# Feed-forward operands made in the stage ahead, half by half; two lead pairs; the position rows written in eight copies

## The chip, the cores and the metric

The kernel runs on one core of one Trainium2 chip. The metric is the device time of one execution in microseconds (us). The kernel before takes 2559.06 us, the median of 3 runs (2556.69 to 2561.37). Below, the engines are PE (matrix products), DVE (VectorE), ACT (ScalarE), POOL (GpSimd) and SP (SyncE, whose queue issues every DMA of this kernel).

## The reference

Two transformer blocks on x of 1024 positions by 1024 channels, in fp32. What the change touches is the end of the first block's cross attention, its feed-forward layer, and two small preparations of the second block that are done beside it:

```python
x = x + o @ w_co                               # cross attention's output projection
h = rmsnorm(x, norm_ffn)
gate, up = split(h @ w_gu, 2)                  # 22 tiles of 128 columns each
x = x + (silu(gate) * up) @ w_down             # hidden width 2816
x = rmsnorm(x, final_norm)
# second block, prepared beside the feed-forward layer:
ada = silu(c) @ ada_w + ada_b                  # 8 vectors of 1024 values
pos_bias = rel_bias[buckets]                   # 16 heads, by distance, masked
```

## The kernel before

Every fp32 product is made as three products of a high and a low part (`wh`/`wl` of the weights, `Xh`/`Xl` or the two `R` of the operand): three matmuls of 128x128 by 128x512. ACT copies the high part, DVE subtracts it for the low part (`split`, and L251/L252 for weights). The 1024 positions are two halves `hf` of 512.

**The co projection** (`g_dense(cow...)`): half 0 for 8 tiles of channels (woven into the cross attention), then half 1. `Residual` adds each result to x (DVE, L1186), squares it on ACT and sums the squares; `rstd()` turns the sum into 1/rms: 4 small matmuls, a power on POOL, 4 matmuls that spread it over the partitions, a copy on ACT (`rf[hf]`).

**Gate and up tile 0** (`g_gu0`) take x times the gain, not yet normalised (`raw_split`, made for half 0 beside the co projection of half 1), and multiply by `rf` when the result is read out.

**Tiles 1 to 21 of gate and up** (`g_fast`) are 21 pairs (gate tile, up tile) by two halves of the input channels and of the positions: a 2x2 block product made with 7 products (A11, A12, S2, S1, S3, A22, S4) of 12 matmuls instead of 8. Their right sides are the blocks B11, B21, B12, B22 of the normalised x and the sums T1 to T4, each split into high and low: `g_operands0`, `g_operands1` (sums on POOL, `right_sums`) and `g_operands2`. Their left sides are weight blocks and their sums (`fast_operand`), made two products ahead per buffer (3 buffers, `ahead`). `load_fast` loads a pair's two weight tiles.

**Beside these products** runs `mods`, one step after each product (`mix`, L1577): first `g_sliding_bias`, then 16 times `g_modulation` (8 loads of `araw`, 8 multiply-adds on DVE into `aacc`, 4 transposes on PE, one reduction). What is left of `mods` after the last product runs by itself (L1578). `g_sliding_bias` makes a table of 16 heads by 384 distances (16 partitions), adds the mask (L1377) and writes every head's row 128 times to `d_bs` in DRAM, in one DMA of 3 MB (L1378). It is read back eight stages later.

`hidden` stores the hidden tiles and their sums in DRAM (`d_h`) for the down projection `dn0` to `dn2`, which has the same 7-product form. Before it, x is loaded again (L1584) and the first third of its operands is fetched and split (`fetch`, `place`).

**What sets the order:** the program is recorded in the order of these generators; a scheduler then places the instructions of each engine's queue by its own estimate of what is ready when. Each engine, and SP's queue, then works in that fixed order and waits at an instruction whose inputs or buffers aren't there. The pool `v` (`vtile2`) has NV = 20 tiles, shared by part of the operands, the hidden tiles and sums, `araw` and `aacc`, and the table of `g_sliding_bias`.

## Time and profile before

| | |
|---|---|
| median of 3 runs | 2559.06 us |
| the profiled execution | 2555.8 us, of it 2553.8 us span |
| PE busy | 2387.7 us (93%) |
| DVE, ACT, POOL busy | 1733.6, 1069.4, 635.6 us |
| DMA | 252.34 MB, 99 GB/s on average |

The profile is of one execution. PE is the engine that is busy nearly all the time, so time that PE stands idle or runs at the lower clock is what a change can take away or add. [...]

### The profile page before, as it was taken

Reading aid. Unit: us, or ns where it says so; the run is one execution under the profiler, and the core shown is the slowest. Engines: PE = TensorE matmul, PEld = TensorE weight load, DVE = VectorE, ACT = ScalarE, POOL = GpSimd, SP = SyncE. Lnnn points to the kernel's source line nnn. Section 1 sums busy time; section 2 is a strip of 40 time slices with the busy share of each in tenths; the row PEclk is TensorE's granted clock in tenths of the full one; section 3 lists DMA queues with packets and bytes.
Section 4 is the critical chain, followed back from the end, with each engine's and each line's share of the span. In section 5 each row is a group of like instructions: output and inputs, shape, how many; then the busy total and the mean of one; then the engine's idle time right before and its main releaser. Section 6 shows DMA issues by size and latency. Waiting matters only on the chain.

```text
span 2553.8 us, 33162 instructions
## 1 busy us (share of the span) xinstructions
PE 2387.7 (93%) x11726; PEld 1976.9 (77%) x11726; DVE 1733.6 (68%) x3238; ACT 1069.4 (42%) x2214; POOL 635.6 (25%) x593
## 2 busy tenths in 40 slices
PE   8899979998997699999699989999999998999997
PEld 7789967777875588888488867888888886788876
DVE  6325667887688577777898675454644658788765
ACT  5214665765653233333344453121221224566652
POOL 4004555534205122221000120000000006544443
PEclk9999988999998899999799989999999999999999
DMA  4322223433242754455754211111111121111123
GB/s 159 95 79 94 63 51 105 123 100 124 73 143 67 172 175 161 158 179 184 275 176 138 75 33 58 42 58 50 43 41 58 50 66 50 59 51 58 60 91 118
DMA packets 122937, 252.34 MB, mean 99 GB/s; under 512 B 21380, under 2 KB 36404, under 8 KB 122772
## 3 DMA queue, kind: packets, MB, share of 16 engines
q1 hardware_dynamic: 122772, 250.24, 31.2%
q8 instruction: 92, 1.51, 0.3%
q14 instruction: 73, 0.60, 0.1%
HBM read 199.84 MB, written 50.33 MB: 98 GB/s over the span
## 4 chain that ended last, share of the span: by engine, by line
PE 77%; DVE 8%; DMA 5%; issue 3%; ACT 3%; POOL 3%; SPq 0%; DVEq 0%; POOLq 0%; ACTq 0%
PE wd L356 11%; PE wd L364 11%; PE wd L363 11%; PE fx L1444 4%; PE fx L1446 4%; PE fx L1445 4%; PE mm L356 2%; PE mm L363 2%; PE mm L364 2%; PE tp L760 2%; PE op L775 2%; PE fz L1444 2%; PE fz L1446 2%; PE fz L1445 2%; DMA wraw<-in_w_in_f 2%
## 5 line engine op out<-in xcount | busy, mean ns | idle before, releaser
L356 PE MATMUL wd<-Xh,wh 128*128 128x512 f32 x756 | 298.7, 396 | 5.1 <-ACT Xh L334 2.1
L364 PE MATMUL wd<-Xl,wh 128*128 128x512 f32 x756 | 295.8, 395 | 7.6 <-DVE Xl L335 7.6
L363 PE MATMUL wd<-Xh,wl 128*128 128x512 f32 x756 | 296.0, 392 | 1.3 <-POOL wl L263 1.3
L263 DVE TENSOR_TENSOR wl<-wraw,wh 128x1024 fp32r<-128x1024 f32 (+1 forms) x121 | 150.5, 1251 | 206.8 <-ACT wh L262 205.9
L262 ACT ACTIVATE wh<-wraw 128x1024 fp32r<-128x1024 f32 (+2 forms) x157 | 158.1, 1013 | 283.7 <-issue 139.6
L428 POOL TENSOR_TENSOR nr<-nv,half 128x4 f32<-128x4 f32 (+1 forms) x25 | 26.7, 1072 | 771.3 <-DVE nv L422 762.1
L1446 PE MATMUL fx<-R,wh 128*128 128x512 f32 x480 | 189.1, 397 | 10.5 <-DVE R L335 10.4
L1444 PE MATMUL fx<-R,wh 128*128 128x512 f32 x480 | 188.6, 398 | 7.8 <-ACT R L334 7.4
L1445 PE MATMUL fx<-R,wl 128*128 128x512 f32 x480 | 190.4, 397 | 0.0
L364 PEld LDWEIGHTS wd<-Xl,wh 128*128 128x128 f32 x756 | 142.6, 189 | 41.6 <-DVE Xl L335 10.0
L356 PEld LDWEIGHTS wd<-Xh,wh 128*128 128x128 f32 x756 | 142.5, 189 | 36.7 <-ACT Xh L334 3.5
L363 PEld LDWEIGHTS wd<-Xh,wl 128*128 128x128 f32 x756 | 142.6, 189 | 33.0 <-POOL wl L263 2.0
L1188 DVE SCALAR_TENSOR_TENSOR x<-wd,ada,x 128x512 f32<-128x512 f32 x144 | 106.4, 748 | 78.0 <-PE wd L364 78.0
L335 DVE TENSOR_TENSOR ptl<-tp,pth 128x512 fp32r<-128x512 f32 (+2 forms) x196 | 122.8, 635 | 50.5 <-ACT pth L334 48.1
L396 POOL TENSOR_TENSOR acc<-acc,sq 128x512 f32<-128x512 f32 (+1 forms) x49 | 72.2, 1475 | 277.4 <-ACT sq L395 265.6
L760 PE MATMUL tp<-ident,p 128*128 128x128 f32 x712 | 122.8, 284 | 11.2 <-POOL p L704 6.8
L334 ACT ACTIVATE pth<-tp 128x512 fp32r<-128x512 f32 (+2 forms) x196 | 106.8, 557 | 54.2 <-PE tp L760 33.9
L1446 PEld LDWEIGHTS fx<-R,wh 128*128 128x128 f32 x480 | 91.3, 190 | 32.4 <-DVE R L335 12.6
L1444 PE MATMUL fz<-R,wh 128*128 128x512 f32 x240 | 95.9, 400 | 21.8 <-DVE c L1555 21.8
L1444 PEld LDWEIGHTS fx<-R,wh 128*128 128x128 f32 x480 | 91.6, 191 | 29.1 <-ACT R L334 8.3
L1400 DVE SCALAR_TENSOR_TENSOR aacc<-araw,cact,aacc 128x512 f32<-128x512 f32 x112 | 95.9, 856 | 25.6 <-DMA araw<-in_ada_w 24.2
L251 ACT ACTIVATE wh<-ws 128x512 fp32r<-128x512 f32 (+1 forms) x132 | 73.8, 584 | 90.5 <-PE fx L1446 62.4
(374 smaller groups left out, 6786.9 us busy)
## 6 DMA issues: line engine op xcount, KB each, us to landing
araw<-in_ada_w SPq DMA_DIRECT2D x128, 256.0 KB, 4.2
wraw<-in_a_w_in SPq DMA_DIRECT2D x34, 512.0 KB, 3.5
hr<-d_h SPq DMA_DIRECT2D x63, 256.0 KB, 4.0
wraw<-in_w_gu SPq DMA_DIRECT2D x23, 512.0 KB, 4.7
sraw<-in_w_gu SPq DMA_DIRECT2D x21, 512.0 KB, 3.6
d_h<-H SPq DMA_DIRECT2D x36, 256.0 KB, 2.7
wraw<-in_a_w_out SPq DMA_DIRECT2D x18, 512.0 KB, 3.5
x<-d_x SPq DMA_DIRECT2D x32, 256.0 KB, 4.8
```

Source lines behind the costliest of these rows:

```text
L262: A.activation(out=wh[:, sl], in_=raw[:, sl], func=AF.Copy)
L263: (G if pool_split[0] else V).tensor_tensor(out=wl[:, sl], in0=raw[:, sl], in1=wh[:, sl].bitcast(F32), op=ALU.subtract)
L334: A.activation(out=h, in_=src, func=AF.Copy)
L335: V.tensor_tensor(out=l, in0=src, in1=h.bitcast(F32), op=ALU.subtract)
L356: ins = T.matmul(ps, lhsT=wh, rhs=xh, start=start, stop=False)
L363: T.matmul(ps, lhsT=wl, rhs=xh, start=False, stop=False)
L364: T.matmul(ps, lhsT=wh, rhs=xl, start=False, stop=stop)
L760: T.transpose(tp[:, (o + j) * 128:(o + j + 1) * 128], b, ident)
L1188: V.scalar_tensor_tensor(out=xt(f, hf), in0=ps, scalar=self.gate(f), in1=xt(f, hf), op0=ALU.mult, op1=ALU.add)
L1444: T.matmul(ps, lhsT=wh[:, sl], rhs=rh[k], start=new and k == 0, stop=False, skip_group_check=not new)
L1445: T.matmul(ps, lhsT=wl[:, sl], rhs=rh[k], start=False, stop=False, skip_group_check=not new)
L1446: T.matmul(ps, lhsT=wh[:, sl], rhs=rl[k], start=False, stop=k == nk - 1, skip_group_check=not new)
```

## The change

- `fast_order(npair, lead)` gives the order of the products; with lead 2 the gate/up stage begins with A11 and A12 of pairs 0 and 1, which need B11 and B21 alone.
- `g_operands0` normalises half 0 of x and makes B11 and B21 beside the co projection of half 1. `g_gu0` uses these for half 0, so half 0's raw split is gone; half 1's raw split and both spills of x follow each result of the co projection. The sum of squares of half 1 goes to POOL.
- T1 and T2 are made on DVE, T3 and T4 on POOL, beside `g_gu0` and the first four products.
- The table of the position rows has a tile of its own (`mk`); NV is 19. Its rows are written two heads at a time, by eight DMAs, recorded ten steps of `mods` apart.
- A step of `mods` after each product and a second one after every third; a modulation has 10 steps instead of 11.
- Beside the last pairs: the first operands of the down projection are fetched and split, and x is loaded again (`done_gu`, `x_again`).

```diff
+    def fast_order(npair, lead=1):
+        seq = [(i, o) for i in range(lead) for o in ("A11", "A12")]
+        for i in range(npair):
+            seq += [(i, o) for o in ("A12", "S2", "S1", "S3") if (i, o) not in seq]
+            if lead <= i + 1 < npair:
                 seq.append((i + 1, "A11"))
+            elif i + 1 < lead:
+                seq.append((i + 1, "S2"))
             seq += [(i, "A22"), (i, "S4")]
...
-                if op == "A12":
-                    load_fast(key[0], key[1] + 1)
+                if op == "A12" and key[1] == 0:
+                    load_fast(key[0], 1)
+                elif op == "S4":
+                    load_fast(key[0], key[1] + 2)
...
-    NV = 20
+    NV = 19
...
+        res.nm[1].eng = G
+        res.raw = lambda f, hf: nc.sync.dma_start(out=d_x[:, f, hs(hf)], in_=xt(f, hf))
...
-        run(weave(g_dense(cow[1], seqB, 4, Xo, res), bg=[g_raw_split(0, gf, X)], every=4))
...
+        mk = ff.tile([16, 384], F32, name="mk")
...
-            V.tensor_tensor(out=bv, in0=psb[:16, :384], in1=bv, op=ALU.add)
-            nc.sync.dma_start(out=d_bs, in_=bv.rearrange("h (o t) -> h o t", o=1).to_broadcast([16, 128, 384]))
+            V.tensor_tensor(out=mk, in0=psb[:16, :384], in1=mk, op=ALU.add)
+        def g_bias_rows():
+            for h in range(0, 16, 2):
+                nc.sync.dma_start(out=d_bs[h:h + 2], in_=mk[h:h + 2].rearrange("h (o t) -> h o t", o=1)
+                                  .to_broadcast([2, 128, 384]))
+                for _ in range(10):
+                    yield 0.0
...
             for k in range(8):
                 norm(k, 0)
-                if k >= 4:
-                    put("B21", k, xt(k, 0))
+                put("B11" if k < 4 else "B21", k, xt(k, 0))
                 yield 0.0
         def g_operands1():
             for k in range(4):
+                b = bs[k]
+                norm(k, 1)
+                b["T1"], b["T2"] = vtile2("T1"), vtile2("T2")
+                V.tensor_tensor(out=b["T1"], in0=b["B12"], in1=b["B11"], op=ALU.subtract)
+                yield 0.0
+                norm(k + 4, 1)
+                V.tensor_tensor(out=b["T2"], in0=b["B22"], in1=b["T1"], op=ALU.subtract)
+                yield 0.0
+                put("T2", k, b["T2"])
                 yield 0.0
...
-        run(mix(g_fast("gu", 21, 4, R, evac_gu), mods, 1))
+        run(weave(g_dense(cow[1], seqB, 4, Xo, res), bg=[g_operands0()], every=3))
+        rf[1] = res.nm[1].rstd()
+        gu0 = g_gu0(H0, [[Tiles(R["B11"][e] + R["B21"][e]) for e in range(2)], X1])
+        run(weave(gu0, bg=[g_operands1()], every=2))
...
+        def done_gu(i, o):
+            if (i, o) in ((19, "S2"), (19, "S3")):
+                fetch(0, ORD[0 if o == "S2" else 1])
+            if i == 20:
+                n = ORD.index(RIGHT[o])
+                place(0, ORD[n], Rs[0])
+                if n + 2 < 7:
+                    fetch(0, ORD[n + 2])
+                if o in ("S1", "A22"):
+                    x_again(8)
+        fast = g_fast("gu", 21, 4, R, evac_gu, done_gu, 2)
+        ops2 = g_operands2()
+        run(mix(take(fast, 4), ops2))
+        run(ops2)
+        for n, u in enumerate(fast):
+            next(mods, None)
+            if n % 3 == 0:
+                next(mods, None)
```

How the built programs stand at the places where this moves work. Names carry the program's buffer numbers; `x4` is a row four times in a row.

SP's queue of DMA issues, where the position rows are written, before (`d_bs` the position rows, `araw` the modulation's inputs, `d_h` stores of hidden tiles, `sraw` gate/up weights):

```order
L1389 DMA araw_8519<-in_ada_w 128x512
L1389 DMA araw_8521<-in_ada_w 128x512
L1584 DMA x_11911<-d_x_98 128x512
L1389 DMA araw_8539<-in_ada_w 128x512
L1389 DMA araw_8563<-in_ada_w 128x512
L1539 DMA d_h_100<-H_8446 128x512
L1378 DMA d_bs_96<-mks_8429 2048x1x384
L1545 DMA d_h_100<-T1_8585 128x512
L200 DMA sraw_8654<-in_w_gu 128x1024
L1539 DMA d_h_100<-H_8577 128x512
```

One DMA writes all 2048 rows, and behind it stand a store and a weight load. The same place in the queue after:

```order
L1381 DMA d_bs_96<-mk_7841 256x1x384
L1394 DMA araw_8512<-in_ada_w 128x512
L1381 DMA d_bs_96<-mk_7841 256x1x384
L1394 DMA araw_8530<-in_ada_w 128x512
L1543 DMA d_h_100<-H_8417 128x512
L1381 DMA d_bs_96<-mk_7841 256x1x384 x6
L1394 DMA araw_8533<-in_ada_w 128x512
L1394 DMA araw_8555<-in_ada_w 128x512
L206 DMA sraw_8748<-in_w_gu 128x1024
```

The eight DMAs of 256 rows are not spread over the stage: two stand an `araw` load apart, and six directly behind each other, with the next two `araw` loads behind all eight.

DVE's queue after, from the third `araw` that it uses to the read-out of pair 0's S1+S4 result (`wl_8693`, `wl_8739` low parts of weights for pairs 2 and 3, `ws` sums of weights, `fz_8466` the result in PSUM):

```order
L1404 SCALAR_TENSOR_TENSOR aacc_8506<-araw_8512,cact_7840,aacc_8506 128x512
L1404 SCALAR_TENSOR_TENSOR aacc_8506<-araw_8530,cact_7840,aacc_8506 128x512
L259 TENSOR_TENSOR wl_8693<-ws_8694,wh_8692 128x512
L259 TENSOR_TENSOR wl_8693<-wraw_8600,wh_8692 128x512
L238 TENSOR_TENSOR ws_8833<-wraw_8600,sraw_8602 128x512
L259 TENSOR_TENSOR wl_8739<-sraw_8449,wh_8738 128x512
L259 TENSOR_TENSOR wl_8739<-ws_8742,wh_8738 128x512
L238 TENSOR_TENSOR ws_8943<-wraw_8600,ws_8792 128x512
L1404 SCALAR_TENSOR_TENSOR aacc_8506<-araw_8533,cact_7840,aacc_8506 128x512
L1564 TENSOR_TENSOR H_8569<-fz_8466,ev_8460 128x512
```

The inputs `araw_8512`, `araw_8530` and `araw_8533` are the three loads in SP's rows above; the read-out `H_8569` stands directly behind the use of `araw_8533`. On PE after, at the end of pair 2's S2 and the start of pair 3's A11:

```order
L1448 MATMUL fx_8636<-R_8242,wh_8640 128x512
L1449 MATMUL fx_8636<-R_8242,wl_8641 128x512
L1450 MATMUL fx_8636<-R_8243,wh_8640 128x512
L1448 MATMUL fx_8810<-R_7892,wh_8692 128x512 [waits DVE_49,Activation_49]
L1449 MATMUL fx_8810<-R_7892,wl_8693 128x512
L1450 MATMUL fx_8810<-R_7893,wh_8692 128x512
```

Pair 3's first product `fx_8810` waits for DVE: the count it waits for is that of `H_8569`, whose PSUM buffer it takes over.

DVE's queue before, in the corresponding place (`mks_8429` the table of position rows, whose buffer the read-out `H_8617` takes over):

```order
L1377 TENSOR_TENSOR mks_8429<-psb_8471,mks_8429 16x384
L1400 SCALAR_TENSOR_TENSOR aacc_8518<-araw_8563,cact_8099,aacc_8518 128x512
L1560 TENSOR_TENSOR H_8577<-fz_8473,ev_8469 128x512
L252 TENSOR_TENSOR wl_8603<-wraw_8495,wh_8602 128x512
L252 TENSOR_TENSOR wl_8603<-sraw_8137,wh_8602 128x512
L252 TENSOR_TENSOR wl_8645<-ws_8646,wh_8644 128x512
L252 TENSOR_TENSOR wl_8645<-wraw_8495,wh_8644 128x512
L231 TENSOR_TENSOR ws_8782<-wraw_8495,ws_8693 128x512
L1560 TENSOR_TENSOR H_8617<-fy_8598,ev_8536 128x512
```

There the third `aacc` of this stretch stands right behind the table's sum, and the read-out `H_8617` is the row that needs the table's buffer. Last, DVE's queue after, at the end of the co projection (`x_6514` its last result, `R` the high and low parts of B11 and B21, `wl_8122` the weights of pair 0):

```order
L1195 TENSOR_TENSOR x_6514<-x_6514,wd_8078 128x512
L1493 SCALAR_TENSOR_TENSOR x_6499<-x_6499,vec_82,rs_7873 128x512
L1493 SCALAR_TENSOR_TENSOR x_6500<-x_6500,vec_82,rs_7873 128x512
L1493 SCALAR_TENSOR_TENSOR x_6501<-x_6501,vec_82,rs_7873 128x512
L1493 SCALAR_TENSOR_TENSOR x_6502<-x_6502,vec_82,rs_7873 128x512
L1493 SCALAR_TENSOR_TENSOR x_6503<-x_6503,vec_82,rs_7873 128x512
L1493 SCALAR_TENSOR_TENSOR x_6504<-x_6504,vec_82,rs_7873 128x512
L1493 SCALAR_TENSOR_TENSOR x_6505<-x_6505,vec_82,rs_7873 128x512
L1493 SCALAR_TENSOR_TENSOR x_6506<-x_6506,vec_82,rs_7873 128x512
L259 TENSOR_TENSOR wl_8122<-wraw_8002,wh_8121 128x512 x2
L344 TENSOR_TENSOR R_7893<-x_6499,R_7892 128x512
```

Before, the low parts of x for half 0 (`Xl`) had all been made ahead of this point; now the eight normalising steps and two low parts of weights stand between the last sum and `R_7893`, the first low part of an operand.

## Rows read from the trace of the kernel before

**Rows 1.** The page's first part: busy us (share) x instructions.

```profile
span 2553.8 us, 33162 instructions
...
PE 2387.7 (93%) x11726; PEld 1976.9 (77%) x11726; DVE 1733.6 (68%) x3238; ACT 1069.4 (42%) x2214; POOL 635.6 (25%) x593
```

**Rows 2.** Windows, four stretches: length, busy (x) per engine, PEclk, DMA share, GB/s.

```profile
777.80:805.00 27.20, 9.36 (x19) 5.68 (x20) 25.39 (x20) 8.30 (x16) 25.28 (x16) 0.56 0.06 19
838.60:866.50 27.90, 6.29 (x16) 4.88 (x16) 7.38 (x12) 2.34 (x5) 0.00 (x0) 0.57 0.95 191
866.50:1234.40 367.90, 367.33 (x1623) 299.54 (x1621) 284.88 (x401) 124.71 (x225) 82.00 (x51) 1.00 0.54 175
1234.40:1265.50 31.10, 7.07 (x22) 5.48 (x23) 24.82 (x37) 6.31 (x10) 1.26 (x1) 0.57 0.93 333
```

**Rows 3.** Waits of PE from 730 to 870: total us, times, longest.

```profile
PE fz L1444 <- DVE c L1555: 21.6, 1, 21.6
PE fx L1446 <- DVE R L335: 10.4, 2, 8.7
PE fx L1444 <- ACT R L334: 7.4, 2, 4.7
```

**Rows 4.** Waits of PE from 1200 to 1290.

```profile
PE adt L1406 <- DVE aacc L1400: 24.2, 3, 10.6
```

**Rows 5.** Timeline of SP from 823: start us, us, issue.

```profile
823.99 0.64 SPq L1378 DMA_DIRECT2D d_bs<-mks  x1
...
858.91 1.72 SPq L1389 DMA_DIRECT2D araw<-in_ada_w  x2
```

**Rows 6.** The tile d_bs: who waited for it, and its landing.

```profile
  DVE H L1560: 26.5, 1
...
DMA to landing us min/median/max: 2.7/2.8/34.9
```

**Rows 7.** Windows while d_bc, then d_bs is written, and after: PEclk, DMA share, GB/s.

```profile
80.00:82.00 2.00, 2.00 (x10) 1.61 (x9) 0.01 (x1) 0.00 (x0) 0.00 (x0) 1.00 0.23 26
845.00:850.00 5.00, 0.00 (x0) 0.00 (x0) 0.00 (x0) 0.00 (x0) 0.00 (x0) 0.50 0.91 99
860.00:865.00 5.00, 4.74 (x11) 3.77 (x12) 4.96 (x9) 1.31 (x3) 0.00 (x0) 0.50 1.04 407
```

**Rows 8.** Timeline of SP from 70: d_bc and the load behind it.

```profile
73.76 0.81 SPq L612 DMA_DIRECT2D d_bc<-bv  x1
75.02 7.29 SPq L213 DMA_DIRECT2D wraw<-in_w_in_f  x1
```

**Rows 9.** Chain of waits from 60 to 135: start us, us, what.

```profile
75.02 33.25 DMA wraw<-in_w_in_f
```

**Rows 10.** The page's sixth part: KB each, us to landing.

```profile
araw<-in_ada_w SPq DMA_DIRECT2D x128, 256.0 KB, 4.2
...
d_h<-H SPq DMA_DIRECT2D x36, 256.0 KB, 2.7
```

**Rows 11.** Timeline of DVE from 753: start us, us, operation x count.

```profile
753.68 5.38 DVE L1493 SCALAR_TENSOR_TENSOR x<-x,vec,rs 128x512 f32<-128x512 f32 x8
...
781.19 6.17 DVE L1493 SCALAR_TENSOR_TENSOR x<-x,vec,rs 128x512 f32<-128x512 f32 x4
```

**Rows 12.** Timeline of POOL from 788.

```profile
788.44 1.71 POOL L1422 TENSOR_TENSOR T<-x 128x512 f32<-128x512 f32 x1
```

**Rows 13.** Lines of DVE by form from 870 to 1210: busy us, mean ns.

```profile
L1400 DVE SCALAR_TENSOR_TENSOR aacc<-araw,cact,aacc 128x512 f32<-128x512 f32 x79 | 68.8, 871 | 19.7 <-DMA araw<-in_ada_w 19.0
...
L1408 DVE TENSOR_REDUCE ada<-adt 128x4 f32<-128x512 f32 x12 | 8.2, 685 | 2.0 <-PE adt L1406 2.0
L1398 DVE TENSOR_SCALAR aacc<-araw,cact 128x512 f32<-128x512 f32 x11 | 7.4, 670 | 1.9 <-DMA araw<-in_ada_w 1.9
```

**Rows 14.** Waits of DVE from 870 to 1210.

```profile
DVE aacc L1400 <- DMA araw<-in_ada_w: 19.0, 15, 3.1
...
DVE wl L252 <- ACT wh L251: 12.2, 9, 2.0
```

## The prediction

> **What bounds the kernel now.** I read the engines' shares first: PE is busy 93% of a span of 2553.8 us [rows 1], so a change pays only where PE stands, runs at the lower clock, or gets fewer matmuls (their number hardly changes). The windows give the full pitch: 1623 matmuls in 367.33 us, .226 us each at clock 1.00 [rows 2]. A hole is what a stretch takes beyond its matmuls at that pitch, so the recovery at the lower clock counts too. The windows show three [rows 2]:

> - A, at 777.8: 27.20 us for 19 matmuls, 27.2 − 19 × .226 = 22.9 lost. PE waits for `R` [rows 3]: DVE's eight normalising steps run ahead of it.
> - B, at 838.6: 27.90 us for 16, 24.3 lost. PE waits 21.6 us for one read-out of DVE [rows 3]. Behind that stands the write of the position rows: issued at 823.99 [rows 5], landed 34.9 us later; the DVE read-out `H` that takes over the table's buffer waits 26.5 us for it [rows 6].
> - C, at 1234.4: 31.10 us for 22, 26.1 lost: the rest of `mods` runs alone, PE waiting 24.2 us for `aacc` [rows 4].

> Together 73 us, which is what the change could win at most.

> **The position rows, the largest term.** In the windows, the write of the position rows (16 source rows) moves 99 GB/s at a DMA share of .91, while other transfers reach 407 GB/s at much the same share [rows 7]: engine time is taken by the many short rows, not by bytes. An earlier write of the same kind, `d_bc`, has 4 source rows: it moves 26 GB/s at a share of .23 [rows 7], which is 3.7 of 16 engines; the 16-row write has 14.6. So it looks as if each source row has one engine, which moves 99/16 = 6.2 to 26/4 = 6.5 GB/s. The `wraw` load issued 1.3 us behind `d_bc` [rows 8] landed only 33.25 us after its issue, as the chain of waits shows [rows 9]; later loads do stand behind such a write, though 12 of 16 engines are free.

> After, each of eight writes has 2 source rows and 2 × 128 × 1536 B = 393,216 B. On 2 engines that takes 393,216/(2 × 6.2 GB/s) = 31.7 us, at 6.5 GB/s 30.2, and by the one write's landing time 34.9 [rows 6]. No row shows which engines a second write gets. If the same two, eight take 8 × 31.5 = 252 us (242 to 279); if different ones, all run side by side and take some 35. I take the same two: `d_bc` and the load behind it show that work isn't dealt to whichever engine is free.

> [...]

> What waits for them: in the built program the eight writes stand nearly back to back in SP's queue, the last six without anything between, and `araw_8533` is the next load behind them. DVE uses it directly ahead of `H_8569`, and PE's `fx_8810`, the first product of pair 3, waits for `H_8569`. So DVE, and through it PE, stand until all eight have landed. In PE's order between 43 and 63 matmuls stand between the table's sum (time t0) and `fx_8810`, 9.7 to 14.2 us; I take 11. The end of the wait: .6 to the issue, 252 for the writes, 2 for the two loads and the store between them (256 KB each, 2.7 to 4.2 us alone [rows 10], but on all engines), 4.2 for `araw_8533` [rows 10], .87 for its `aacc` [rows 13] and .7 for `H_8569`: t0 + 260.4. PE stands 260.4 − 11 = 249.4. To this come 3 for the lower clock after it (13 matmuls at half the pitch; B shows the clock at .50 while PE runs again at 860 [rows 7]), and 3 for an echo: `araw_8588`, a few places on, stands behind stores that need POOL's sums (1.71 [rows 12]) and land in 2.7, then loads 4.2. B after: 255; against 24.3, **+231** (+222 to +258).

> **Operands made in the stage ahead.** Hole A's cause goes: half 0 is normalised beside the co projection. But `rf[0]` is late: in DVE's order all eight normalising steps and two low parts stand between the last sum of that projection and `R_7893`, which PE needs for its next products. From the end of the last co product: two sums, two low parts and one `R` at about .67 (the plain 128x512 form [rows 13]), 3.35, and 5.38 for the eight steps [rows 11], 8.7 us; PE has 12 wide and a few small matmuls to run in it, 3.0. That is 5.7 lost. POOL's last sums, 8 at 1.71 [rows 12], come beside the four lead products instead of ahead of all; A11 and A12 of two pairs cover 48 × .226 = 10.8 us of 13.7, up to 2.9 late, and up to 3 at the lower clock. I take 9.5 after: 9.5 − 22.9 = **−13** (−18 to −8; the lower end if the eight steps overlap the co products).

> **Rest of `mods` and x.** With four steps for three products, and 10 steps in a modulation instead of 11, 16 modulations need 160 steps plus three, done after 122 of the 147 products. Both x and the first down operands are fetched beside the last pairs. Hole C is left with the change of buffers: 5 (0 to 15), **−21** (−26 to −11).

> **The price of the faster rate.** A modulation costs DVE 7 × .871 + .670 + .685 = 7.45 us [rows 13]; per product .677 before, 7.45 × (4/3)/10 = .993 after, +.316. Before, the stretch has 1623/12 = 135 products of 2.73 us, in which DVE works 284.88/135 = 2.11 [rows 2]; after 2.43. Waits that end in DVE, 19.0 for `araw` and 12.2 for ACT in 340 us [rows 14], are .25 a product more: 2.68 of 2.73. DVE is then full, but not over. For 122 products at no cost the term is 0; if the waits double for the one buffer less (NV 19), 122 × .2 = 24. I take **+10**, since a queue this full passes on part of its waits. The T1 and T2 sums on DVE and the squares on POOL lie beside PE's products and cost nothing, as PE is busy throughout them; uncovered, four T1 and four T2 would be 8 × .67 = 5.4.

> **Sum.** The profiled execution is 2555.8, 3.3 below the median of the runs. 2555.8 + 231 − 13 − 21 + 10 = 2762; on the median's footing +3, **2765 us**, 8% slower.

> **Rivals.**
> 1. The eight writes go to different engines, or are spread over all, and take together what the one takes. For: 3 MB at 99 GB/s is 32 us, and the other 14 engines are free. Against: `d_bc`'s .23, and the load that waited behind it. Then the end is t0 + .6 + 34.9 + 4.2 + .87 + .7 = t0 + 41.3, PE stands 30, with clock and echo 36: B is +12 and the sum 2555.8 + 12 − 13 − 21 + 10 = 2544, on the median's footing 2547. Faster by .5%; same or slower if the faster rate costs its 24 (2561). Chance .10.
> 2. The writes are slow, but loads issued later aren't held behind them. Then B goes away altogether, −24: 2555.8 − 24 − 13 − 21 + 10 = 2508, median's footing 2511. Against: 33.25 us for a load behind `d_bc` [rows 9]. Chance .04.
> 3. The change doesn't win A and C: DVE is full throughout, the sums of the operands come late, and the stage runs at DVE's 2.43 + .5 = 2.93 a product, 122 × .2 = 24 more, with A and C at their low ends. On top of the slow writes: 2555.8 + 231 − 8 − 11 + 24 = 2792, footing 2795. It decides from .05 us more DVE wait per product on. Chance .12.

> **How the numbers follow.** My forecast has .74, and rival 3, slower too, .12; together .86. Low ends of the four terms are +222 − 18 − 26 + 0 = +178 (2737), high ends +258 − 8 − 11 + 24 = +263 (2822). The lower rows of all terms at once are unlikely, but each engine's rate is known to some 5% only (12 us), so the range runs from 2722 to 2830. It leaves out rivals 1 and 2 (.14) and little else. A measurement here can tell .2%, about 5 us, from no change. Faster: most of rival 1 and all of 2, .12; same .02; slower .86.

> **What the profile after would show.** Right: one wait of PE of some 250 us, ended by DVE's `H`, and a wait of DVE for `araw` of about the same length; during it a DMA share near .12 and 13 GB/s; landing times of `d_bs` growing by about 31 us from one piece to the next. The A hole has shrunk to under 12 us, and no stretch of PE waiting for `aacc` is left near the down projection. Wrong: pieces that land about 35 us after issue all alike (rival 1), `araw` landing in 4 us while `d_bs` is still under way (rival 2), or products of 2.9 us with DVE busy throughout (rival 3).

## The result, and the profile after

The changed kernel takes 2619.86 us (median of 4 runs, 2619.08 to 2620.89), the kernel before 2558.18 in the same comparison: a ratio of 1.024, interval 1.0222 to 1.0257. It is 62 us slower; the forecast was 206 us slower. The direction, the place and the chain of the loss are as forecast, the size of its largest term is not: it was put at more than twice what came.

The page's first part after; PE's busy time is that of [rows 1], the span 63.4 us longer:

```profile
span 2617.2 us, 33160 instructions
...
PE 2386.9 (91%) x11726; PEld 1978.1 (76%) x11726; DVE 1716.2 (66%) x3229; ACT 1062.0 (41%) x2206; POOL 636.6 (24%) x592
```

PE's waits from 700 to 975 (total us, times, longest; those over 3 us) hold one that is new, and two small ones where [rows 3] had 10.4 and 7.4:

```profile
PE fx L1448 <- DVE H L1564: 116.1, 1, 116.1
PE wd L365 <- ACT R L343: 4.1, 1, 4.1
PE fx L1449 <- DVE wl L259: 3.8, 2, 2.8
```

DVE's waits from 830 to 960; this is what PE's long wait goes back to:

```profile
DVE aacc L1404 <- DMA araw<-in_ada_w: 116.8, 3, 90.2
```

And SP's queue there (start us, us that the issue or issues took, issue). `d_bs` are the eight writes, x6 the last six of them:

```profile
820.51 0.73 SPq L1381 DMA_DIRECT2D d_bs<-mk  x1
821.35 5.64 SPq L1394 DMA_DIRECT2D araw<-in_ada_w  x1
827.04 1.83 SPq L1381 DMA_DIRECT2D d_bs<-mk  x1
828.98 12.59 SPq L1394 DMA_DIRECT2D araw<-in_ada_w  x1
841.62 1.83 SPq L1543 DMA_DIRECT2D d_h<-H  x1
843.50 75.86 SPq L1381 DMA_DIRECT2D d_bs<-mk  x6
919.46 17.87 SPq L1394 DMA_DIRECT2D araw<-in_ada_w  x2
```

The rows say that SP is held at its own issues: 12.59 us at an `araw` behind the second write, 75.86 us at the six, 17.87 at the loads behind them. Only then is `araw_8533` on its way, and DVE's third use of `araw` in this stretch waits 90.2 us. PE stops at 834.3 and goes on at 950.4.

The windows after (us, busy of PE, PEld, DVE, ACT, POOL, clock, DMA share, GB/s; the clock, PEclk, is the one granted to PE: matmuls follow each other at .226 us at 1.00 [rows 2], at .43 at .50 [rows 7]): the two places of hole A, hole B with a piece of its inside, what follows it, and the rest of the stage.

```profile
740.00:762.00 22.00, 17.93 (x65) 13.94 (x65) 20.05 (x26) 13.49 (x23) 8.24 (x6) 0.77 0.25 84
788.00:802.00 14.00, 11.23 (x43) 8.73 (x42) 14.00 (x19) 8.84 (x17) 4.90 (x3) 0.88 0.09 29
833.00:953.00 120.00, 3.87 (x12) 2.88 (x11) 7.91 (x12) 2.38 (x4) 1.95 (x2) 0.52 0.16 37
860.00:910.00 50.00, 0.00 (x0) 0.00 (x0) 0.00 (x0) 0.00 (x0) 0.00 (x0) 0.50 0.13 25
953.00:975.00 22.00, 18.27 (x74) 14.34 (x74) 13.00 (x20) 4.65 (x8) 5.63 (x5) 0.91 0.62 203
975.00:1310.00 335.00, 332.83 (x1473) 270.54 (x1472) 275.42 (x394) 115.84 (x209) 82.57 (x49) 1.00 0.60 194
```

From 860 to 910, during the writes, the DMA share is .13, two engines of 16, as forecast; but they move 25 GB/s, where I had 12.4 to 13. At 25 GB/s a piece of 393,216 bytes takes 15.7 us, and eight take 126.

### The profile page after: what moved, and what is told of

It is laid out like the page before. It is cut to its first block, busy times and chain, and to the rows that moved or that the text cites. A ratio compares the mean times of both kernels' runs of the same rounds, so it can differ in the third digit from the quotient of the medians.

```text
span 2617.2 us, 33160 instructions
## 1 busy us (share of the span) xinstructions
PE 2386.9 (91%) x11726; PEld 1978.1 (76%) x11726; DVE 1716.2 (66%) x3229; ACT 1062.0 (41%) x2206; POOL 636.6 (24%) x592
## 4 chain that ended last, share of the span: by engine, by line
PE 74%; DVE 8%; DMA 5%; issue 3%; POOL 3%; SPq 3%; ACT 3%; POOLq 0%; DVEq 0%; ACTq 0%
PE wd L365 11%; PE wd L372 11%; PE wd L373 11%; PE fx L1449 3%; PE fx L1448 3%; PE fx L1450 3%; SPq L1381 3%; DMA araw<-in_ada_w 3%; PE mm L365 3%; PE mm L373 2%; PE mm L372 2%; PE tp L769 2%; PE op L784 2%; PE fz L1448 2%; PE fz L1450 2%
## 5 line engine op out<-in xcount | busy, mean ns | idle before, releaser
L365 PE MATMUL wd<-Xh,wh 128*128 128x512 f32 x740 | 293.1, 397 | 5.1 <-ACT Xh L343 2.1
L373 PE MATMUL wd<-Xl,wh 128*128 128x512 f32 x740 | 289.9, 395 | 7.5 <-DVE Xl L344 7.5
L1448 PE MATMUL fx<-R,wh 128*128 128x512 f32 x480 | 188.8, 397 | 116.8 <-DVE H L1564 116.1
L372 PE MATMUL wd<-Xh,wl 128*128 128x512 f32 x740 | 290.6, 393 | 1.3 <-POOL wl L272 1.3
L1448 PEld LDWEIGHTS fx<-R,wh 128*128 128x128 f32 x480 | 91.3, 190 | 137.7 <-issue 116.5
L405 POOL TENSOR_TENSOR acc<-acc,sq 128x512 f32<-128x512 f32 (+1 forms) x56 | 83.2, 1488 | 280.3 <-ACT sq L404 267.8
L769 PE MATMUL tp<-ident,p 128*128 128x128 f32 x712 | 122.5, 284 | 11.4 <-POOL p L713 6.8
L1449 PEld LDWEIGHTS fx<-R,wl 128*128 128x128 f32 x480 | 91.3, 190 | 25.8 <-DVE wl L259 5.2
L769 PEld LDWEIGHTS tp<-ident,p 128*128 128x128 f32 x712 | 88.6, 145 | 26.1 <-POOL p L713 7.7
```

The costliest lines, as they stand in the source:

```text
L365: ins = T.matmul(ps, lhsT=wh, rhs=xh, start=start, stop=False)
L372: T.matmul(ps, lhsT=wl, rhs=xh, start=False, stop=False)
L373: T.matmul(ps, lhsT=wh, rhs=xl, start=False, stop=stop)
L769: T.transpose(tp[:, (o + j) * 128:(o + j + 1) * 128], b, ident)
L1448: T.matmul(ps, lhsT=wh[:, sl], rhs=rh[k], start=new and k == 0, stop=False, skip_group_check=not new)
L1449: T.matmul(ps, lhsT=wl[:, sl], rhs=rh[k], start=False, stop=False, skip_group_check=not new)
```

## The experiments

All are edits of the changed kernel but one; times are medians, ratios are to the kernel before in the same comparison (its median lay between 2556 and 2567), with the 95% interval.

**One write of 16 rows in place of eight.**

```diff
-            for h in range(0, 16, 2):
-                nc.sync.dma_start(out=d_bs[h:h + 2], in_=mk[h:h + 2]...to_broadcast([2, 128, 384]))
+            nc.sync.dma_start(out=d_bs, in_=mk...to_broadcast([16, 128, 384]))
```

> The changed kernel, with the position rows written in one DMA of 16 source rows (as before) instead of eight of 2; nothing else differs. Theory: the eight writes are the whole loss. One write took 31.7 us at 99 GB/s before, so PE's wait of 116 us becomes some 30 (36 with clock and echo), and the gains at the other two places remain: about 2540 to 2550 us, .5% faster than before. Rival (the writes are only in the way of something else that is slow, such as DVE's full queue): stays over 2590.

2534.0 us, .988 (.985 to .991), below what was expected. The eight writes are more than the whole loss: without them the change is 1% faster than before. PE's wait is now this one:

```profile
PE fx L1446 <- DVE H L1562: 27.5, 1, 27.5
```

**Four writes of four rows, near and apart.** `d_bs[4 * j:4 * j + 4]` from `mk[4 * j:4 * j + 4]`, and `d_bs[j:16:4]` from `mk[j:16:4]`, for j from 0 to 3:

> The changed kernel, with four writes of 4 neighbouring source rows instead of eight of 2. In the changed kernel two rows moved 25 GB/s together (12.5 each), before four rows of another table 26 (6.5 each) and sixteen 99 (6.2 each). Theory N (neighbours share: four neighbouring source rows, or the four engines that serve them, move 25 GB/s together, whether two or four of them are busy): each write takes 31 us, all four 126, as the eight did: 2610 to 2630 us. Theory E (a row's engine moves 12.5 GB/s and d_bc was slow for a reason of its own): 50 GB/s, 63 us in all, about 2557 us.

> As the run with four writes, but each takes source rows j, j+4, j+8, j+12, so that no two rows of one write are neighbours (the rows in DRAM are then as far apart too). Theory N with the source partitions sharing: 12.5 GB/s a row or more, 50 GB/s, 63 us in all or less: 2530 to 2560 us. Theory N with the engines sharing (4 source rows are the same four engines whatever the rows): 126 us, 2610 to 2630. Theory E: about 2557 us, as the run with neighbours would be.

Near: 2611.7 us, 1.019 (1.015 to 1.022). Apart: 2530.1 us, .986 (.983 to .989). The windows while the writes run (columns as above), near, then apart:

```profile
840.00:855.00 15.00, 0.00 (x0) 0.00 (x0) 0.00 (x0) 0.00 (x0) 0.00 (x0) 0.50 0.23 25
```

```profile
836.00:848.00 12.00, 0.00 (x0) 0.00 (x0) 2.65 (x4) 0.00 (x0) 0.00 (x0) 0.51 0.26 100
```

The shares are .23 and .26 of 16: four engines in both, and the same bytes. Near they move 25 GB/s together, apart 100. Theory E and the sharing of engines both fall; an engine alone moves 25 GB/s, a fourth of the 100 (the expectation for apart counted on 12.5 or more), and what is shared belongs to the rows.

**Which side's rows.** The four source rows apart and the four blocks in DRAM near (`d_bs[4 * j:4 * j + 4]` from `mk[j:16:4]`), and the reverse:

> Four writes as in the runs before, each from source partitions j, j+4, j+8, j+12 into four neighbouring blocks of DRAM (so heads land in other heads' places; same bytes, same count). Theory P (four neighbouring source partitions share 25 GB/s): 100 GB/s as with both sides apart, 2525 to 2535 us. Theory D (the blocks in DRAM, 192 KB apart, get in each other's way): 25 GB/s, about 2612 us.

> The reverse: each of four writes from four neighbouring source partitions into blocks of DRAM that are four heads apart (heads in other heads' places again). Theory P: 25 GB/s, about 2612 us. Theory D: 100 GB/s, 2525 to 2535 us.

Source apart: 2529.2 us, .988 (.985 to .991). Source near: 2614.6 us, 1.022 (1.019 to 1.025). Theory P, on both. In the first, SP is through with the last two writes (timeline, columns as above) in 7.85 us, where the run with both sides near took 28.74; in the second the window, with some loads in it, shows about the old rate:

```profile
836.01 7.85 SPq L1381 DMA_DIRECT2D d_bs<-mk  x2
```

```profile
868.26 28.74 SPq L1381 DMA_DIRECT2D d_bs<-mk  x2
```

```profile
840.00:860.00 20.00, 0.00 (x0) 0.00 (x0) 2.56 (x4) 0.00 (x0) 0.00 (x0) 0.50 0.23 29
```

So it is the source partitions: four neighbours give 25 GB/s between them, however many engines read them.

**Where the groups begin.** Five writes, of rows 2 to 5, 6 to 9, 10 to 13, 0 to 1 and 14 to 15:

> The changed kernel with five writes of neighbouring source rows, 2 to 5, 6 to 9, 10 to 13, then 0 to 1 and 14 to 15. Theory A (the sharing groups are partitions 0 to 3, 4 to 7 and so on): the first three straddle two groups each, 50 GB/s, 15.7 us each, and the last two 15.7 each: 79 us in all instead of 126, about 2565 to 2578 us. Theory B (any four neighbours share): 31 us each for the first three, 126 in all, 2608 to 2620 us.

2575.3 us, 1.008 (1.006 to 1.010): theory A. Within these 16 partitions the groups are 0 to 3, 4 to 7, 8 to 11 and 12 to 15; others were not tried. PE's wait there:

```profile
PE fx L1448 <- DVE H L1564: 69.5, 1, 69.5
```

**The table on 128 partitions.** Each head's row is made on 8 neighbouring partitions, and each partition writes 16 of its 128 copies:

```diff
-        mk = ff.tile([16, 384], F32, name="mk")
+        mk = ff.tile([128, 384], F32, name="mk")
+        rb2 = ff.tile([32, 16], F32, name="rb2")
...
+            nc.sync.dma_start(out=mk, in_=I["k_mks"].rearrange("h (o t) -> h o t", o=1).to_broadcast([16, 8, 384]))
+            V.tensor_copy(out=oh[0:32, 384:512].rearrange("b (h o) -> b h o", o=8),
+                          in_=rb2.rearrange("b (h o) -> b h o", o=1).to_broadcast([32, 16, 8]))
...
+            T.matmul(psb[:, :384], lhsT=oh[0:32, 384:512], rhs=oh[0:32, 0:384], start=True, stop=True)
...
+            nc.sync.dma_start(out=d_bs.rearrange("h (o r) t -> (h o) r t", o=8),
+                              in_=mk.rearrange("p (r t) -> p r t", r=1).to_broadcast([128, 16, 384]))
```

> The changed kernel, with the table of position rows made on 128 partitions (each head on 8 neighbouring partitions; one copy on DVE and wider loads added) and written in one DMA, 16 times from each partition. Theory N with the partitions sharing: every group of 4 partitions moves 25 GB/s and no longer decides; 16 engines at 12.5 GB/s or more, 200 GB/s, 16 us instead of 32: 2525 to 2535 us. Theory N with the engines sharing, or writes of 1536 bytes as such being slow: 99 GB/s again, as the run with one write, 2540 to 2550 us.

2513.4 us, .979 (.977 to .982), below what was expected. The windows of the write and of the rest of the stage, and what is left of PE's wait:

```profile
829.00:836.00 7.00, 6.92 (x31) 5.32 (x29) 1.97 (x4) 1.68 (x4) 0.00 (x0) 1.00 1.02 338
850.00:1210.00 360.00, 354.17 (x1564) 287.05 (x1563) 293.65 (x423) 125.77 (x227) 85.71 (x52) 1.00 0.58 194
```

```profile
PE fx L1450 <- DVE H L1566: 7.1, 1, 7.1
```

338 GB/s with the loads beside it. The same table and write alone, in the kernel before:

> The kernel before, with nothing changed but the table of position rows on 128 partitions and written in one DMA from there. Theory: its write goes from 35 to about 9 us, and PE's wait of 21.6 us at that place (24.3 with the clock) goes with it, nothing else: 2532 to 2542 us. Rival (the operands made earlier and the end of mods were worth nothing, and the run at 2513 owed all to the write): 2510 to 2518 us.

2534.1 us, .990 (.986 to .993), as expected. The longest landing of `d_bs`, that of the write, was 34.9 us in [rows 6]; now:

```profile
DMA to landing us min/median/max: 2.6/2.7/9.6
```

Of before's waits of PE, that of 21.6 us [rows 3] is gone and the others stand; so the write was worth 24 us there, and the rest of the change is worth the step from 2534 to 2513:

```profile
PE adt L1410 <- DVE aacc L1404: 24.3, 3, 10.7
PE fx L1450 <- DVE R L335: 10.4, 2, 8.7
PE fx L1448 <- ACT R L334: 7.4, 2, 4.7
```

**The eight writes kept where they are recorded** (`tc.keep_in_program_order` round each issue), first from 2 rows each, then from the wide table, two of its 16 copies each:

> The changed kernel, with its eight writes of 2 source rows kept where they are recorded, ten steps of mods apart, instead of six behind each other. Theory: each holds the loads behind it for 15.7 us; PE ran 12 us on after the first in the changed kernel, so each costs some 15.7 + 4 + 2 - 12, about 8 us and a little clock, eight times: 2555 to 2590 us. Rival (buffers hide each of them, so that the order alone was the fault): 2503 to 2515 us.

> The changed kernel with the table on 128 partitions, written in eight DMAs that are kept where they are recorded, ten steps of mods apart (each takes two of the sixteen repeats from every partition, 384 KB, at some 350 GB/s 1.1 us). Theory: the 7.1 us that PE still waited with the one wide write, and its time at the lower clock, go: 2501 to 2508 us. Rival (that wait is DVE's full queue or the araw loads themselves): 2511 to 2516 us, as with one write.

From 2 rows: 2605.7 us, 1.020 (1.018 to 1.021), worse than expected. Spread out, they hold loads in eight places instead of one (SP is held 12.02 to 19.75 us at the `araw` issues behind each), and PE waits again and again (waits of PE from 800 to 1300):

```profile
PE fx L1448 <- DVE H L1570: 29.9, 3, 11.1
PE adt L1411 <- DVE aacc L1404: 23.8, 7, 10.4
PE fz L1449 <- DVE wl L259: 14.9, 2, 7.9
PE fx L1448 <- DVE H L1564: 9.9, 1, 9.9
```

With two smaller ones of 4.0 and 3.0 us these make some 85 us; so the order in SP's queue, which I had read as the cause, changes little. From the wide table: 2506.7 us, .980 (.977 to .983), within what was expected; its ratio can't be told from that of one wide write.

**The eight writes on POOL's queue** (`nc.gpsimd.dma_start`):

> The changed kernel, with its eight writes of 2 source rows issued from POOL's queue instead of SP's. Theory (a load waits because it stands behind the writes in SP's queue): loads pass them, PE's wait of 116 us goes, and what is left are POOL's sums behind its eight issues: 2505 to 2545 us. Rival (a load waits because two of the engines that carry it are busy, whichever queue the writes are in): 2600 to 2620 us.

2548.5 us, .997 (.996 to .999): neither. The window from 822, the writes (issues, KB each, median us to landing) and PE's waits:

```profile
822.00:845.00 23.00, 10.53 (x46) 8.26 (x44) 5.72 (x9) 2.53 (x5) 4.85 (x5) 0.78 0.83 118
```

```profile
d_bs<-mk POOLq DMA_DIRECT2D x8, 384.0 KB, 44.2
```

```profile
PE adt L1411 <- DVE aacc L1404: 25.2, 3, 24.1
PE fx L1448 <- DVE H L1564: 19.8, 1, 19.8
```

From this queue the writes run side by side, and with the loads .83 of the engines are busy; yet all DMA together moves 118 GB/s, not far from the one write of 16 rows (99 [rows 7]). That fits four groups of partitions at 25 each. But they land 44.2 us after their issue, later than the one write (34.9 [rows 6]), and the run is slower than the one with that write (.997 against .988); why, no run here shows. POOL itself stands 27.2 us before its eighth issue, with its sums behind. PE still waits 24.1 us for `aacc`, which uses the `araw` loads, although these stand in another queue; that the loads are late, and wait for the engines that the writes hold up, some 13 (.83 of 16), is argued and not shown.

**What closed the hole behind the last product.** The wide write with one step of `mods` a product, as before:

> The run with one wide write (2513 us), with one step of mods after each product instead of four for three. Theory: the faster rate costs nearly nothing while it lasts (PE's pitch in the stage is .2274 us after, .2267 before) and is what closes the hole behind the last product: 163 steps against 143 products leave 20 to run alone, some 20/32 of the 26 us of before: about 16 us slower, 2525 to 2533 us. Rival (the faster rate costs 10 us as predicted, and the down operands hide the rest): 2503 to 2510 us.

2506.8 us, .982 (.980 to .983). By the ratios this can't be told from the faster rate (.979), and it isn't the 16 us slower that the theory asked for. The rival's figure holds, but not its reason; the windows of the stage and of the time behind it:

```profile
850.00:1210.00 360.00, 355.22 (x1557) 289.01 (x1557) 292.42 (x406) 126.66 (x230) 86.06 (x52) 0.99 0.55 185
1210.00:1300.00 90.00, 86.43 (x377) 69.11 (x376) 86.84 (x158) 36.65 (x72) 1.89 (x1) 1.00 0.75 255
```

```profile
PE adt L1413 <- DVE aacc L1406: 0.5, 1, 0.5
```

From 850 to 1210 PE is busy 355.22 us here and 354.17 at the faster rate (above): the rate costs nothing that these rows show. And `mods` run on to 1269 beside the down products, which wait .5 us for `aacc`. Two more runs undo the early fetch of the down operands and of x (`done_gu`), at the faster and at the old rate:

```diff
-        fast = g_fast("gu", 21, 4, R, evac_gu, done_gu, 2)
+        fast = g_fast("gu", 21, 4, R, evac_gu, None, 2)
...
         R.clear()
+        x_again(16)
+        fetch(0, ORD[0])
+        fetch(0, ORD[1])
+        for n, b in enumerate(ORD):
+            place(0, b, Rs[0])
+            if n + 2 < 7:
+                fetch(0, ORD[n + 2])
```

> The run with one wide write (2513 us; four steps of mods for three products), with the first operands of the down projection and x fetched after the last product, as before. Theory F (the early fetch alone closes the hole, since the down products can run over whatever is left of mods): mods are done by then, but PE has no operand until a load, a split and the stores ahead of them are through: 10 to 25 us slower, 2523 to 2538 us. Theory M (the hole was mods, and these are done): 2510 to 2517 us.

> The run with the old rate of mods and one wide write (2507 us), with the first operands of the down projection and x fetched after the last product, as before: both parts that bear on that hole are undone. Theory F: the hole is back as in the kernel before, 26 us: 2528 to 2540 us, and only this run has PE waiting for aacc there. Theory M: 20 steps of mods alone instead of 32, 16 us: 2520 to 2526 us.

At the faster rate 2521.2 us, .985 (.982 to .988), 8 us over the run with the fetch, with intervals that just miss each other; at the old rate 2525.6 us, .988 (.985 to .991), 19 over. The first lies between the ranges of the two theories, the second in that of theory M, though, as theory F had it, only here PE waits long for `aacc`. PE's longest waits there, first the faster rate, then the old:

```profile
PE fx L1450 <- ACT R L343: 2.0, 1, 2.0
```

```profile
PE adt L1413 <- DVE aacc L1406: 17.8, 3, 10.0
```

Windows of PE alone at that place (busy, clock, DMA share, GB/s): with both parts, with the early fetch alone, with the faster rate alone, with neither:

```profile
1190.00:1300.00 110.00, 110.00 (x478) 1.00 0.62 209
1190.00:1300.00 110.00, 106.43 (x464) 1.00 0.76 259
1190.00:1300.00 110.00, 105.93 (x454) 1.00 0.62 207
1190.00:1300.00 110.00, 91.93 (x393) 0.92 0.68 227
```

Either part alone removes all but .5 us of the wait for `aacc` and most of the hole: PE stands 0, 3.6, 4.1 and 18.1 us in these rows. With the early fetch the faster rate is worth 3.6 us at most, which the medians can't show.

**Together.** Wide table, eight writes kept ten steps apart, old rate:

> The table on 128 partitions, written in eight DMAs that are kept ten steps apart, with the old rate of mods. If what the wide write still cost (about 7 us) and the adt waits of the kept order (4 us) go together: 2498 to 2506 us; if not, 2505 to 2512 us as with either alone.

2504.8 us (2503.6 to 2505.1), .979 (.976 to .982). It beats both kernels, by 4.4% the changed one; from the run with one wide write it can't be told apart by the ratios.

## Why the prediction was wrong

| term | forecast | measured | from |
|---|---|---|---|
| position rows (B) | +231 | +98 | 117.3 lost in 833 to 953, 5.3 in 953 to 975, less 24.3 |
| operands (A) | −13 | about −7 | 11.4 + 4.3 lost, less 22.9 |
| end of `mods`, x (C) | −21 | −26 | no wait left there |
| faster rate | +10 | +1 | 975 to 1310: 335 − 1473 × .2267 |
| sum | +207 | +66 | span: +63.4 |

Lost time is counted as in the prediction, a window less its matmuls at the full pitch; in 740 to 762 only 47 of the 65 are wide, so A's term is an upper bound of what remained. The sum of the windows misses the span by 3 us, which I can't place.

**The step that failed** is the rate of a write with two source rows: "each source row has one engine, which moves 99/16 = 6.2 to 26/4 = 6.5 GB/s". The first half is right: shares of .13, .23 and .91 go with 2, 4 and 16 rows. The second isn't: an engine alone moves 25 GB/s, and 6.2 was a quarter of that, because in both writes that the trace of before shows, the rows come in fours that share one source of 25 GB/s. Rows on the same four partitions were the only ones there were, so 16 rows (four groups, 99) and 4 rows (one group, 26) fitted both readings; two rows in one group share 25 by two. The runs with four rows near and apart told them apart in one step: four engines in both, 25 against 100 GB/s. They also answer "engine time is taken by the many short rows": the rows of 1536 bytes are the same in both, at four times the rate.

With 15.7 us a piece the prediction's own sum gives 8 × 15.7 = 126 in place of 252, B at +105 and 2640 us. The smaller price of the rate (9 less) and of C (5 less), with A's 6 the other way, make that 2632, and the 7 us by which B was less, 2625: PE ran 13.8 us beyond the table's sum (it ends at 820.48) where I took 11, and DVE's use of `araw_8533` begins 128.3 us behind that sum, not .6 + 126 + 2 + 4.2 = 132.8; so the loads cost less than I had counted. The 5 us that are left to the measured 2620 are no more than the 3 that I can't place and the spread of the executions.

```profile
948.78 0.75 DVE L1404 SCALAR_TENSOR_TENSOR aacc<-araw,cact,aacc 128x512 f32<-128x512 f32 x1 [90.16 <-DMA araw<-in_ada_w]
```

Why four neighbouring source partitions share 25 GB/s, no run here shows.

**The rest, point by point.** The eight writes run one after another on two engines (share .13 from 860 to 910, SP held for 75.86 us); that these are always the same two, no view here shows. So rival 1, which would have them run side by side, fell on SP's queue. On POOL's, where they did, the run came to 2548.5 us, near rival 1's 2547; that is in part luck, since the writes took longer than its 34.9 us and other terms differed too. Rival 2 (loads pass the writes) fell on SP's queue, where DVE waited 116.8 us for `araw`; on POOL's no row shows whether they passed, and PE still waited 24.1 us for `aacc`. Rival 3 (DVE too full) fell: PE keeps its pitch with `mods` at either rate (354.17 and 355.22 us busy in 360). The chain from `araw_8533` over `H_8569` to `fx_8810` stood as read from the queues. The landing times that were to grow by 31 us can't be read: the trace gives none for these writes, and SP's issues show the pace instead.

Hole A was misread in part. The eight normalising steps of half 0 end at 759.06 in the trace of before, well ahead of the hole at 777.8; the steps inside it are half 1's, 4.76 and 6.17 us for four each, beside POOL's sums ([rows 11], and this row of before, which waits for half 1's `rs`):

```profile
775.91 4.76 DVE L1493 SCALAR_TENSOR_TENSOR x<-x,vec,rs 128x512 f32<-128x512 f32 x4 [1.88 <-ACT rs L441]
```

After, the hole left 15.7 us where I took 9.5. PE's wait at the end of the co projection is 4.1 us, less than the 5.7 that I had, although the eight steps took 7.12 us, not 5.38. More than I allowed went behind that wait, where PE ran at a clock of .54: 10.80 us for 21 wide and 8 narrow matmuls, 6.1 lost. In the second place PE waits 2.8 us for DVE's `wl`, not for POOL's sums. The rows after (timeline of DVE, window):

```profile
749.05 7.12 DVE L1493 SCALAR_TENSOR_TENSOR x<-x,vec,rs 128x512 f32<-128x512 f32 x8 [0.65 <-ACT rs L450]
```

```profile
751.20:762.00 10.80, 10.79 (x29) 8.15 (x30) 10.80 (x16) 8.61 (x15) 1.11 (x1) 0.54 0.00 0
```

The order in SP's queue, to which I gave the whole wait, is not the fault either: in the recorded places the writes cost nearly as much (2605.7 us against 2619.9).

## What to carry to other kernels

A transfer's rate is to be taken from a row with the same source partitions, not scaled by the count of rows or engines: the .23 and .26 windows have four engines each, and the second moves four times as much (100 against 25 GB/s). Where a small table is copied out many times, make it on all partitions first (here one DVE copy and a wider product took the write's landing from 34.9 to 9.6 us, 3 MB at over 300 GB/s), and only then think of splitting the DMA or moving it in the queue. When a rate is inferred from two writes that differ in two things at once, keep the other reading's rate in the range: 25 GB/s for a group gives 2640, and the range began at 2722.
